# Sparse attention in one stream of a two-model program: scores from row halves of the array, values stationary, features on partitions

## The chip, the cores and the metric

The program runs on one core of a Trainium2 chip. The metric is the device time of one execution in microseconds (us). The kernel before took 1988.86 us in the median of 3 runs (1982.52 to 1991.17).

The engines by the names that the profile uses: PE is the matrix engine (PEld is its weight load), DVE the vector engine, ACT the scalar engine, POOL the general engine, SP the queue that issues most loads. PSUM is the memory that PE writes, in banks of 512 fp32 columns by 128 partitions.

## The reference

Two transformer blocks run one after the other on 256 tokens of width 1024. The second block has two layers, and in each of them three mixers read the same input: a gated linear attention, an RWKV recurrence and a sparse attention with 8 query heads and 2 key groups of 4 heads each. Their outputs, 256, 256 and 512 wide, stand side by side and are multiplied by `w_out`. Cut to what matters, the sparse attention is

```
o = gate0 * softmax(q k_cmp) v_cmp        # 15 compressed keys per group
  + gate1 * softmax(q k_s, causal) v_s    # "s"
  + gate2 * softmax(q k_w, causal) v_w    # "w"
```

With 256 tokens both of the last two branches are plain causal attention over all keys, so "s" and "w" are the same work on other keys and values. Head dimension is 64.

## The kernel before

Everything is kept in fp32. A product with a weight matrix is done in three matmuls on operands split in a high and a low part; products inside the mixers are true fp32 matmuls, which the trace shows as two passes each. The kernel is written with named pools of tiles, and a scheduler puts the instructions of all streams of a stage into one fixed order per engine; each engine then works strictly through its list and waits where an operand isn't ready. So the three mixers of a layer are woven into one list of PE instructions, and a stage of a layer ends with the product with `w_out` (`dense`, lines 215 to 217).

The stage is called "m2" in the table `SCOPES`: it gives the number of buffers of each tag, per stream (R is RWKV, G the gated attention, N the sparse attention), and the PSUM banks. Score banks of N are the two banks "d", which `dense` uses too; the transposed probabilities go through "n" for the first 128 tokens and "q" for the others; sums of the values go to the one bank "o".

The names that matter here:

- `nsa_in` makes the keys `N["kT"]`: 64 features of group 0 on partitions 0 to 63 and of group 1 on 64 to 127. The tile has a block of columns for each group, in which the other group's partitions are zero (`fill`), so that a whole-array matmul of the stacked queries of two heads with both blocks gives two heads' scores.
- `nsa_half` (line 1750) works on one half h of the tokens (128 queries). First comes the compressed branch: probabilities, transposed, times `vc`, in one matmul of 512 columns (line 1781), copied to `acc`.
- Then, for "s" and "w", it goes over groups of heads that fill one score bank: 4 heads of 128 keys in the first half, 2 heads of 256 keys in the second. Scores and the causal mask (a bf16 identity times a mask) go to the bank, DVE takes the maximum (line 556), ACT the exponentials with their sums (line 1802). `probs_T` transposes the unnormalised probabilities (line 750) and copies them to SBUF (line 118); each head's transposed block is then the stationary operand of a matmul with 64 columns of values. These last are the `po` rows of line 473; line 473 is the helper `Chain`, which keeps matmuls into one bank in order.
- When all 8 heads are done, DVE divides by the sums and multiplies by the gate (lines 1809, 1810, 1812), and POOL adds the result to `acc` (line 1813).
- `self.result` transposes `acc` (line 229) and splits it in high and low part (lines 232, 233), the operand of the product with `w_out`.

Of the kernel before, what the change touches and what calls it, by code (L numbers as in the profile page):

```python
# [18 lines left out]
AF = mybir.ActivationFunctionType  # L19
OP = mybir.AluOpType  # L20
# [8 lines left out]
class Core:  # L29
# [18 lines left out]
                     tC2="pC2", aC3="pC3", tC3="pC3", oO="o")),  # L48
        "m2": (dict(lb4R=1, s=11, op=3, ol=2, lb2N=5, lb2R0=3, lb2R1=3, b2R0=1, b2R1=1, lb4N=1, b05R=4, b05G=3, b05N=3, lb05N=2,
                     lb4G=2, b2G=5, lsR=5, lsG=1, lsN=1, sR=8, sG=6, sN=11, b1R=5, b1G=2, b1N=2, b2R=5, b2N=5, lb2G=8, lb2R=12),  # L50
                dict(g=1, r=2, q=1, aR0="r", tR0="r", aR1="q", tR1="g", n=1, o=1, d=2, aR="r", tR="r", oR="r", aG="g", tG="g",
# [946 lines left out]
class Mix2(Mix1):  # L998
# [108 lines left out]
    def mixer2(self, layer):  # L1107
        nc, I = self.nc, self.I
        get = self.norm_T(self.x, None)
        put, oget = self.operand(8, [("lb2G", 2), ("lb2R", 2), ("op", 4)])  # L1110

        self.result = lambda h, b0, nb, y: self.split_T(y, nb, lambda b, m: put(h, b0 + b, m))
        w = I["w_in_2"][layer]
        self.N = {}
        with self.on("N"):
            self.nsa_queries(get, w)
        for s, f, g in (("R", self.rwkv_in, self.rwkv), ("G", self.gla_in, self.gla), ("N", self.nsa_in, self.nsa)):
            with self.on(s):
                f(layer, get, w)
                with self.later(800 if s == "G" else 0):  # L1120
                    g(layer)

        def product(done):
            for n0 in (0, 512):
                self.dense(oget, I["w_out_2"][layer], n0, 512, lambda h, ps: done(h, n0, ps), order=(0, 2, 3, 1), apart=(("op", "ol"), None, ("lb4R", "lb4G"), None) if n0 else ())
        self.post("ln1", layer, "lb2R", product)
# [492 lines left out]
    def nsa_in(self, layer, get, w):  # L1619
        nc, I = self.nc, self.I  # L1620
        N = self.N

        kT = self.l(1024)
        self.fill(kT, 0.0)
        N["kT"] = kT.rearrange("p (n g t) -> p n g t", n=2, g=2)
        vs = self.l(512)
# [13 lines left out]
        def keys_T(h, src, j):  # L1640
            ro = rotated(h, src)
            pt = self.p("t")
            nc.tensor.transpose(pt[:, :128], ro, self.ident)
            for g in range(2):
                self.evac(N["kT"][64 * g:64 * g + 64, j, g, h * 128:(h + 1) * 128], pt[64 * g:64 * g + 64, :128])

# [103 lines left out]
    def nsa_half(self, h, kc, vc):  # L1750
# [27 lines left out]
        nc.tensor.transpose(pt[:, :128], pr, self.ident)  # L1778
        self.evac(pT, pt[:, :128])
        po = self.p("o")  # L1780
        nc.tensor.matmul(po, pT, vc, start=True, stop=True)
        acc = self.t(512)
        self.evac(acc, po)

        nk = 128 * (h + 1)
        per = 512 // nk
        for j, n in enumerate("sw"):
            po = self.p("o")
            och = Chain(self)
            sums = self.t(8)  # L1790
            for a in range(0, 8, per):

                heads = [(c // 2, c % 2) for c in range(a, a + per)]
                ps, sv, nmax, pr, pv = self.open_scores(per, nk)
                ch = Chain(self)
                for i in range(0, per, 2):
                    ch(sv[:, i:i + 2], qv[:, heads[i][0]], N["kT"][:, j, :, :nk], stop=False)
                    ch(sv[:, i:i + 2, nk - 128:], self.ident_b, self.cb["causal"][:, None, :].to_broadcast([128, 2, 128]), start=False)
                self.largest(sv, nmax)
                for i, (c, g) in enumerate(heads):  # L1800
                    c += 4 * g
                    nc.scalar.activation(pv[:, i], sv[:, i], AF.Exp, bias=nmax[:, i:i + 1], accum_out=sums[:, c:c + 1])
                pT = self.probs_T(h, [pv[:, i] for i in range(per)])
                for i, (c, g) in enumerate(heads):
                    s = slice((4 * g + c) * 64, (4 * g + c) * 64 + 64)
                    for b in range(h + 1):
                        och(po[:, s], pT[i, b], N["v"][n][b][:, rows(g)], start=(b == 0), stop=(b == h))
            r = self.t(8)
            nc.vector.reciprocal(r, sums)
            nc.vector.tensor_tensor(r, r, gate[:, :, 1 + j], op=OP.mult)  # L1810
            tmp = self.t(512)
            nc.vector.tensor_tensor(eight(tmp), eight(po), r[:, :, None].to_broadcast([128, 8, 64]), op=OP.mult)
            nc.gpsimd.tensor_tensor(acc, acc, tmp, op=OP.add)
        self.result(h, 4, 4, acc)


class Net(Mix2):
# [32 lines left out]
    "rwkv_g2_2", "rwkv_k_k_2", "rwkv_k_a_2", "rwkv_r_k_2", "rwkv_ln_w_2", "rwkv_ln_b_2", "nsa_pos_k_2",  # L1850
    "nsa_pos_v_2", "nsa_wk1_2", "nsa_wk2_2", "nsa_wv1_2", "nsa_wv2_2", "w_out_2", "ln1_w_2", "ln1_b_2",
    "ffn_w_down_2", "ln2_w_2", "ln2_b_2",
# [3 lines left out]
def gate_up(g, u):  # L1856
# [4 lines left out]
    both = both.transpose(*range(n), n + 3, n, n + 2, n + 1, n + 4, n + 5, n + 6)  # L1861
    return np.ascontiguousarray(both).reshape(*both.shape[:n + 3], 1024)


# [30 lines left out]
```

## Time and profile before

| what | value |
|---|---|
| median of 3 runs | 1988.86 us |
| the profiled execution, its own time | 1985.36 us |
| its span | 1983.7 us |
| PE busy | 1906.5 us (96%) |
| DVE busy | 1257.2 us (63%) |
| ACT busy | 1005.7 us (51%) |
| POOL busy | 191.4 us (10%) |
| granted TensorE clock, mean | 0.993 |

The span runs from the first instruction to the last; the time of the execution has 1.7 us around it. Time of a PE instruction is read from the start of one row to the start of the next, since its own duration holds a tail that overlaps the next one's start. In a row such as `128*64 128x128 f32` the first pair is the part of the array in use (rows by columns), the second the output. The stage of layer 0 whose order changes lies between about 1232 and 1352 us, that of layer 1 between about 1652 and 1773 us.

### The profile page before, as it was taken

Reading aid. Unit: us, or ns where it says so; the run is one execution under the profiler, and the core shown is the slowest. Engines: PE = TensorE matmul, PEld = TensorE weight load, DVE = VectorE, ACT = ScalarE, POOL = GpSimd, SP = SyncE. Lnnn points to the kernel's source line nnn. Section 1 sums busy time; section 2 is a strip of 40 time slices with the busy share of each in tenths; the row PEclk is TensorE's granted clock in tenths of the full one; section 3 lists DMA queues with packets and bytes.
Section 4 is the critical chain, followed back from the end, with each engine's and each line's share of the span. In section 5 each row is a group of like instructions: output and inputs, shape, how many; then the busy total and the mean of one; then the engine's idle time right before and its main releaser. Section 6 shows DMA issues by size and latency. Waiting matters only on the chain.

```text
span 1983.7 us, 34147 instructions
## 1 busy us (share of the span) xinstructions
PE 1906.5 (96%) x13548; PEld 1698.5 (86%) x13548; DVE 1257.2 (63%) x2007; ACT 1005.7 (51%) x1607; POOL 191.4 (10%) x270
## 2 busy tenths in 40 slices
PE   8999999899999999898999999998999999998998
PEld 7997788799989987677999788877998787878996
DVE  5665865766566656676666557666555767576555
ACT  5544655555445545665554445543454455444542
POOL 0000401000000001320000012310000213210000
PEclk9999999999999999999999999999999999999999
DMA  7666443466656656234566654313666745025664
GB/s 239 194 214 214 140 149 105 126 195 195 197 192 193 195 189 191 94 108 138 171 192 194 201 150 126 110 44 120 199 192 191 184 143 158 1 86 176 197 191 138
DMA packets 158641, 319.09 MB, mean 161 GB/s; under 512 B 28944, under 2 KB 49681, under 8 KB 158481
## 3 DMA queue, kind: packets, MB, share of 16 engines
q1 hardware_dynamic: 157888, 315.79, 51.6%
q8 instruction: 106, 1.74, 0.4%
q0 software_dynamic: 160, 0.52, 0.1%
q10 hardware_dynamic: 432, 0.60, 0.1%
q14 instruction: 55, 0.44, 0.1%
HBM read 315.82 MB, written 1.05 MB: 160 GB/s over the span
## 4 chain that ended last, share of the span: by engine, by line
PE 51%; issue 4%; DVE 3%; ACT 1%; DMA 0%; SPq 0%; POOL 0%; DVEq 0%; POOLq 0%; ACTq 0%
PE pd L473 23%; PE pd L216 5%; PE pd L215 5%; PE pd L217 5%; PE po L473 2%; PE ppC L473 1%; DVE wl L158 1%; PE pg L1240 1%; PE pg L473 1%; PE pt L509 0%; PE pr L1516 0%; PE pq L1516 0%; PE pq L1525 0%; PE pt L229 0%; PE pq L1521 0%
## 5 line engine op out<-in xcount | busy, mean ns | idle before, releaser
L158 DVE TENSOR_TENSOR wl<-wr,wh 128x1024 fp32r<-128x1024 f32 (+2 forms) x557 | 677.3, 1218 | 390.2 <-PE pd L473 133.9
L157 ACT ACTIVATE wh<-wr 128x1024 fp32r<-128x1024 f32 (+2 forms) x557 | 584.6, 1051 | 552.9 <-PE pd L473 206.9
L473 PE MATMUL pd<-opX,wl 128*128 128x256 f32 x2112 | 584.3, 277 | 2.2 <-DVE s L241 1.0
L473 PE MATMUL pd<-olX,wh 128*128 128x256 f32 x2112 | 584.4, 277 | 0.3 <-DVE olX L233 0.2
L473 PE MATMUL pd<-opX,wh 128*128 128x256 f32 x2112 | 583.7, 277 | 0.0
L473 PEld LDWEIGHTS pd<-opX,wl 128*128 128x128 f32 x2112 | 397.4, 188 | 3.1 <-ACT opX L232 2.2
L473 PEld LDWEIGHTS pd<-olX,wh 128*128 128x128 f32 x2112 | 397.8, 188 | 0.7 <-DVE olX L233 0.7
L473 PEld LDWEIGHTS pd<-opX,wh 128*128 128x128 f32 x2112 | 397.6, 188 | 0.0
L216 PE MATMUL pd<-wl,op 128*128 128x512 f32 (+5 forms) x984 | 375.6, 382 | 3.3 <-DVE wl L158 3.1
L217 PE MATMUL pd<-wh,op 128*128 128x512 f32 (+5 forms) x984 | 372.1, 378 | 0.0
L215 PE MATMUL pd<-wh,ol 128*128 128x512 f32 (+5 forms) x984 | 354.4, 383 | 3.0 <-DVE ol L233 1.7
L216 PEld LDWEIGHTS pd<-wl,op 128*128 128x128 f32 x984 | 185.5, 189 | 38.3 <-DVE wl L158 5.8
L215 PEld LDWEIGHTS pd<-wh,ol 128*128 128x128 f32 x984 | 184.6, 188 | 37.7 <-DVE ol L233 1.9
L217 PEld LDWEIGHTS pd<-wh,op 128*128 128x128 f32 x984 | 185.6, 189 | 32.5
L350 DVE TENSOR_TENSOR b<-pd,b 128x256 f32<-128x256 f32 x132 | 55.9, 424 | 62.2 <-ACT b L349 44.2
L242 POOL TENSOR_TENSOR ls<-s,cf 128x1 f32<-128x1 f32 (+2 forms) x30 | 25.4, 848 | 721.5 <-DVE s L241 721.5
L242 POOL TENSOR_TENSOR s<-s,cf 128x1 f32<-128x1 f32 (+2 forms) x22 | 23.0, 1048 | 428.3 <-DVE s L241 426.9
L473 PE MATMUL pd<-op,wl 128*128 128x256 f32 x208 | 58.5, 281 | 5.9 <-DVE lb2R L1316 4.4
L349 ACT ACTIVATE b<-b 128x256 f32<-128x256 f32 x88 | 36.8, 418 | 46.6 <-DVE b L348 46.6
L473 PE MATMUL pd<-ol,wh 128*128 128x256 f32 x208 | 58.1, 279 | 0.0
L473 PE MATMUL pd<-op,wh 128*128 128x256 f32 x208 | 57.9, 278 | 0.0
L354 DVE TENSOR_TENSOR ol<-b,op 128x512 fp32r<-128x512 f32 x66 | 45.4, 688 | 18.0 <-ACT op L353 18.0
(513 smaller groups left out, 2272.9 us busy)
## 6 DMA issues: line engine op xcount, KB each, us to landing
wr<-in_ffn_gu_dram SPq DMA_DIRECT2D x264, 512.0 KB, 4.1
wr<-in_ffn_w_down_dram SPq DMA_DIRECT2D x132, 512.0 KB, 3.6
wr<-in_w_in_dram SPq DMA_DIRECT2D x45, 512.0 KB, 4.5
wr<-in_ab_w_in_dram SPq DMA_DIRECT2D x24, 512.0 KB, 4.0
wr<-in_xm_w_kv_dram SPq DMA_DIRECT2D x16, 512.0 KB, 3.6
wr<-in_w_out_dram SPq DMA_DIRECT2D x16, 512.0 KB, 3.7
wr<-in_ab_w_out_dram SPq DMA_DIRECT2D x8, 512.0 KB, 3.5
wr<-in_xm_w_q_dram SPq DMA_DIRECT2D x8, 512.0 KB, 4.0
```

The lines of the kernel that those rows point to most:

```text
L157: nc.scalar.activation(hi, raw, AF.Copy)
L158: nc.vector.tensor_tensor(lo, raw, hi.bitcast(F32), op=OP.subtract)
L215: nc.tensor.matmul(o, xl, wh[:, k], start=first, stop=False)
L216: nc.tensor.matmul(o, xh, wl[:, k], start=False, stop=False)
L217: nc.tensor.matmul(o, xh, wh[:, k], start=False, stop=last)
L242: self.pow = nc.gpsimd.tensor_tensor(r, a, self.mhalf[:, :n], op=OP.pow)
L349: nc.scalar.activation(s, s, AF.Silu)
L350: nc.vector.tensor_tensor(y[:, b * 256:b * 256 + 256], ps[:, 256:], s, op=OP.mult)
L354: nc.vector.tensor_tensor(lo, yv, hi.bitcast(F32), op=OP.subtract)
L473: i = self.k.nc.tensor.matmul(out, lhsT, rhs, start=start, stop=stop, skip_group_check=skip)
L1240: nc.tensor.matmul(ps[rows(n), 4 * h + 2 * a:4 * h + 2 * a + 2], z[:, a, s], zq[:, a, :, s], start=True, stop=True)
```

## The change

- `nsa_in` no longer fills a zeroed tile for the keys: the tile holds 64 features of group 0 and of group 1 on the two halves of the partitions, and one copy writes it.
- Scores: for each head one matmul with 64 rows of the array (its group's half), 128 or 256 columns, in place of one whole-array matmul for two heads. Two score banks are opened, one for each group.
- The probabilities are divided by their sums and multiplied by the gate before they are transposed (`weigh`, a DVE product of 512 columns), with a reciprocal and a product of 2 or 4 sums for each bank.
- Values are the stationary operand, 64 columns of the array (the half of the group), and the transposed probabilities move, 512 or 256 columns at a time. All three branches add into one bank "o" whose partitions are features; `acc`, the product at the end of each branch, the POOL additions and the four transposes of `result` are gone. The bank is split into high and low part directly (`split`).
- The rows of `w_out` are put in the order of the new operand when the inputs are laid out.
- The table gives N one more buffer of two kinds and drops the 1024-wide one.

In the new file the lines of `nsa_half` move: line 1811 is the transpose that was line 750, and lines 1805, 1806 and 697 the reciprocal, the product of the sums and `weigh`.

```diff
-        "m2": (dict(lb4R=1, s=11, op=3, ol=2, lb2N=5, lb2R0=3, lb2R1=3, b2R0=1, b2R1=1, lb4N=1, b05R=4, b05G=3, b05N=3, lb05N=2,
-                     lb4G=2, b2G=5, lsR=5, lsG=1, lsN=1, sR=8, sG=6, sN=11, b1R=5, b1G=2, b1N=2, b2R=5, b2N=5, lb2G=8, lb2R=12),
+        "m2": (dict(lb4R=1, s=11, op=3, ol=2, lb2N=6, lb2R0=3, lb2R1=3, b2R0=1, b2R1=1, b05R=4, b05G=3, b05N=3, lb05N=2,
+                     lb4G=2, b2G=5, lsR=5, lsG=1, lsN=1, sR=8, sG=6, sN=11, b1R=5, b1G=2, b1N=2, b2R=5, b2N=6, lb2G=8, lb2R=12),
...
-        kT = self.l(1024)
-        self.fill(kT, 0.0)
-        N["kT"] = kT.rearrange("p (n g t) -> p n g t", n=2, g=2)
+        N["kT"] = self.l(512).rearrange("p (n t) -> p n t", n=2)
...
-            for g in range(2):
-                self.evac(N["kT"][64 * g:64 * g + 64, j, g, h * 128:(h + 1) * 128], pt[64 * g:64 * g + 64, :128])
+            self.evac(N["kT"][:, j, h * 128:(h + 1) * 128], pt[:, :128])
...
         po = self.p("o")
-        nc.tensor.matmul(po, pT, vc, start=True, stop=True)
-        acc = self.t(512)
-        self.evac(acc, po)
+        pov = po.rearrange("p (i t) -> p i t", i=4)
+        och = Chain(self)
+        for i in range(4):
+            for g in range(2):
+
+                och(pov[rows(g), i], vc[:, (4 * g + i) * 64:(4 * g + i) * 64 + 64], pT, start=(i == 0), stop=False, skip=True)
...
-            for a in range(0, 8, per):
-
-                heads = [(c // 2, c % 2) for c in range(a, a + per)]
-                ps, sv, nmax, pr, pv = self.open_scores(per, nk)
-                ch = Chain(self)
-                for i in range(0, per, 2):
-                    ch(sv[:, i:i + 2], qv[:, heads[i][0]], N["kT"][:, j, :, :nk], stop=False)
-                    ch(sv[:, i:i + 2, nk - 128:], self.ident_b, self.cb["causal"][:, None, :].to_broadcast([128, 2, 128]), start=False)
-                self.largest(sv, nmax)
-                for i, (c, g) in enumerate(heads):
-                    c += 4 * g
-                    nc.scalar.activation(pv[:, i], sv[:, i], AF.Exp, bias=nmax[:, i:i + 1], accum_out=sums[:, c:c + 1])
-                pT = self.probs_T(h, [pv[:, i] for i in range(per)])
-                for i, (c, g) in enumerate(heads):
-                    s = slice((4 * g + c) * 64, (4 * g + c) * 64 + 64)
-                    for b in range(h + 1):
-                        och(po[:, s], pT[i, b], N["v"][n][b][:, rows(g)], start=(b == 0), stop=(b == h))
-            r = self.t(8)
-            nc.vector.reciprocal(r, sums)
-            nc.vector.tensor_tensor(r, r, gate[:, :, 1 + j], op=OP.mult)
-            tmp = self.t(512)
-            nc.vector.tensor_tensor(eight(tmp), eight(po), r[:, :, None].to_broadcast([128, 8, 64]), op=OP.mult)
-            nc.gpsimd.tensor_tensor(acc, acc, tmp, op=OP.add)
-        self.result(h, 4, 4, acc)
+            for a in range(0, 4, per):
+                S = [self.open_scores(per, nk) for g in range(2)]
+                chains = [Chain(self) for g in range(2)]
+                for i in range(per):
+                    for g in range(2):
+                        chains[g](S[g][1][:, i], qv[rows(g), a + i], N["kT"][rows(g), j, :nk], start=(i == 0), stop=False, skip=True)
+                st = []
+                for g, (ps, sv, nmax, pr, pv) in enumerate(S):
+                    chains[g](sv[:, :, nk - 128:], self.ident_b, self.cb["causal"][:, None, :].to_broadcast([128, per, 128]),
+                              start=False, skip=True)
+                    self.largest(sv, nmax)
+                    sums = self.t(per)
+                    for i in range(per):
+                        nc.scalar.activation(pv[:, i], sv[:, i], AF.Exp, bias=nmax[:, i:i + 1], accum_out=sums[:, i:i + 1])
+                    nc.vector.reciprocal(sums, sums)
+                    nc.vector.tensor_tensor(sums, sums, gate[:, 4 * g + a:4 * g + a + per, 1 + j], op=OP.mult)
+                    self.weigh(pv, sums)
+                    pt = self.p("t")
+                    st.append(self.t(512))
+                    for m, (b, i) in enumerate((b, i) for b in range(h + 1) for i in range(per)):
+                        nc.tensor.transpose(pt[:, m * 128:(m + 1) * 128], pv[:, i, b * 128:(b + 1) * 128], self.ident)
+                    self.evac(st[-1], pt)
+                for b in range(h + 1):
+                    for g in range(2):
+                        och(pov[rows(g), a:a + per], N["v"][n][b][:, rows(g)], st[g][:, b * per * 128:(b + 1) * per * 128],
+                            start=False, stop=(n == "w" and b == h), skip=True)
+        self.split(self.put, h, 4, pov)
```

The order of the instructions changes in the second part of the two m2 stages alone, and there on PE, DVE, ACT and POOL; SP's list is the same. PE's list in layer 0, second half of the tokens, branch "w", before: `pd` with 512 columns are the scores, `pd<-cb` the mask, `pq` the transposes of the probabilities, `po` the products with the values, `pr` another stream.

```order
L473 MATMUL pd_14641<-lb4N_14011,lb2N_12395 128x512
L473 LDWEIGHTS cb
L473 MATMUL pd_14641<-cb 128x2x128
L1469 MATMUL pr_13432<-lb2R_12988,lb2R_12991 64x64 x8
L473 MATMUL po_14601<-lb2N_14013,b2N_14612 128x64 x4
L750 MATMUL pq_14630<-cf,b2N_14623 128x128 x4
L473 MATMUL pd_14660<-lb4N_14011,lb2N_12395 128x512
L473 LDWEIGHTS cb
L473 MATMUL pd_14660<-cb 128x2x128
L473 MATMUL po_14601<-lb2N_14013,b2N_14631 128x64 x4
L750 MATMUL pq_14649<-cf,b2N_14642 128x128 x4
```

PE's list at the same place, after: `pd_14638` and `pd_14641` are the score banks of group 0 and group 1, `pq_14612` and `pq_14627` the transposes of the two banks before.

```order
L473 MATMUL pd_14638<-lb2N_14008,lb2N_12392 128x256 x2
L473 LDWEIGHTS cb
L473 MATMUL pd_14638<-cb 128x2x128
L1811 MATMUL pq_14612<-cf,b2N_14595 128x128 x4
L473 MATMUL po_14497<-b2N_14613,lb2N_14009 64x256
L473 MATMUL pd_14641<-lb2N_14008,lb2N_12392 128x256 x2
L473 LDWEIGHTS cb
L473 MATMUL pd_14641<-cb 128x2x128
L1811 MATMUL pq_14627<-cf,b2N_14598 128x128 x4
L473 MATMUL po_14497<-b2N_14628,lb2N_14009 64x256
L473 MATMUL po_14497<-b2N_14613,lb2N_14009 64x256
L473 MATMUL po_14497<-b2N_14628,lb2N_14009 64x256
```

The scores of the two groups stand apart, with mask, transposes and a product with values between them, and each `po` row that reads a tile (`b2N_14613`, `b2N_14628`) stands right behind the transposes that fill it. Before, a score, its mask or another stream's work stood between.

PE's list where the stage of layer 0 ends, before: `po` is the last product with values, `pq<-cf` the transposes of `acc`, `pd` the product with `w_out` for the first (`pd_14702`) and second half of the tokens (`pd_14703`), `op` and `ol` the operand from N.

```order
L473 MATMUL po_14601<-lb2N_14013,b2N_14669 128x64 x4
L215 MATMUL pd_14703<-wh_14706,lb2G_12391 128x512
L216 MATMUL pd_14703<-wl_14707,lb2G_12388 128x512
L217 MATMUL pd_14703<-wh_14706,lb2G_12388 128x512
L215 MATMUL pd_14703<-wh_14706,lb2G_12391 128x512
L216 MATMUL pd_14703<-wl_14707,lb2G_12388 128x512
L217 MATMUL pd_14703<-wh_14706,lb2G_12388 128x512
L229 MATMUL pq_14685<-cf,b2N_14515 128x128 x4
L216 MATMUL pd_14702<-wl_14743,op_12390 128x512
```

And after (`pd_14694` and `pd_14695` are the two halves now):

```order
L217 MATMUL pd_14694<-wh_14734,op_12387 128x512
L215 MATMUL pd_14694<-wh_14752,lb2R_12389 128x512
L473 MATMUL po_14497<-b2N_14672,lb2N_14009 64x256
L473 MATMUL po_14497<-b2N_14657,lb2N_14009 64x256
L473 MATMUL po_14497<-b2N_14672,lb2N_14009 64x256
L215 MATMUL pd_14695<-wh_14716,ol_12390 128x512
L216 MATMUL pd_14695<-wl_14717,op_12387 128x512
L217 MATMUL pd_14695<-wh_14716,op_12387 128x512
```

The transposes are gone, and the first row behind the last product reads the low part of that product's own result.

## Rows read from the trace of the kernel before

**Rows 1.** The page: span, and busy time of each engine.

```profile
span 1983.7 us, 34147 instructions
PE 1906.5 (96%) x13548; PEld 1698.5 (86%) x13548; DVE 1257.2 (63%) x2007; ACT 1005.7 (51%) x1607; POOL 191.4 (10%) x270
```

**Rows 2.** Stretches: length, busy PE, PEld, DVE, ACT, POOL (instructions), clock, DMA.

```profile
1232.50:1284.00 51.50, 51.50 (x499) 42.39 (x499) 35.20 (x86) 28.45 (x60) 17.39 (x26) 1.00 0.35 112
1303.00:1344.00 41.00, 39.98 (x327) 29.89 (x327) 29.19 (x102) 17.92 (x52) 6.81 (x6) 1.00 0.17 53
1724.00:1765.00 41.00, 39.98 (x326) 29.81 (x326) 29.39 (x103) 18.26 (x52) 6.79 (x6) 1.00 0.16 52
```

**Rows 3.** PE in order of time: start, length, instruction [idle before, releaser].

```profile
1277.32 0.60 PE L473 MATMUL pd<-lb4N,lb2N 128*128 128x256 f32 x2
1277.75 0.27 PE L473 MATMUL pd<-cb 128*128 128x256 bf16 x1
...
1316.30 1.10 PE L473 MATMUL po<-lb2N,b2N 128*128 128x64 f32 x8 [0.71 <-ACT b2N L118]
1317.24 0.61 PE L750 MATMUL pq<-cf,b2N 128*128 128x128 f32 x4
1317.69 1.02 PE L473 MATMUL pd<-lb4N,lb2N 128*128 128x512 f32 x2
1318.55 0.27 PE L473 MATMUL pd<-cb 128*128 128x256 bf16 x1
1318.66 1.00 PE L473 MATMUL po<-lb2N,b2N 128*128 128x64 f32 x8
1319.50 0.61 PE L750 MATMUL pq<-cf,b2N 128*128 128x128 f32 x4
```

**Rows 4.** The same view, a block in which two row halves work.

```profile
1190.39 0.48 PE L1381 MATMUL pr<-b1R,b1R 64*128 64x256 f32 x1
1190.40 0.48 PE L1382 MATMUL pr<-lb2R,b1R 64*128 64x256 f32 x1
1190.71 0.38 PE L1381 MATMUL pr<-b1R,b1R 64*128 64x256 f32 x1
...
1191.15 0.38 PE L1382 MATMUL pr<-lb2R,b1R 64*128 64x256 f32 x1
1191.46 0.39 PE L473 MATMUL pd<-ol,wh 128*128 128x256 f32 x1
```

**Rows 5.** The same view, blocks of column halves and whole array in turn.

```profile
1284.83 1.09 PE L1240 MATMUL pg<-lb4G,b2G 128*64 128x128 f32 x16
1285.86 1.10 PE L1543 MATMUL pr<-b1R,lb2R 128*128 128x64 f32 x8
1286.89 0.66 PE L1548 MATMUL pr<-lb2R,lb2R 128*64 128x128 f32 x8
1287.48 1.16 PE L1525 MATMUL pq<-lb2R,b2R 128*128 128x128 f32 x8
```

**Rows 6.** The same view, the end of the stage in layer 0.

```profile
1343.09 1.10 PE L473 MATMUL po<-lb2N,b2N 128*128 128x64 f32 x8 [0.31 <-ACT b2N L118]
...
1346.40 0.66 PE L229 MATMUL pq<-cf,b2N 128*128 128x128 f32 x4 [0.75 <-POOL b2N L1813]
1347.48 0.50 PE L216 MATMUL pd<-wl,op 128*128 128x512 f32 x1 [0.42 <-DVE wl L158]
```

**Rows 7.** Single lines: duration in ns, least/median/most, first and last start.

```profile
L697 DVE TENSOR_TENSOR b2C<-b2C,sC x20: 684/692/694, 372.4 to 936.6; 128x512 f32<-128x512 f32 x20
L1809 DVE RECIPROCAL sN<-sN x8: 195/202/204, 1291.7 to 1760.7; 128x8 f32<-128x8 f32 x8
L1810 DVE TENSOR_TENSOR sN<-sN,lb05N x8: 158/162/166, 1292.7 to 1761.1; 128x8 f32<-128x8 f32 x8
L1812 DVE TENSOR_TENSOR b2N<-po,sN x8: 691/692/692, 1297.3 to 1765.1; 128x512 f32<-128x512 f32 x8
L118 ACT ACTIVATE b2N<-pq x8: 590/597/602, 1315.7 to 1342.4; 128x512 f32<-128x512 f32 x8
```

More of the change, by code (lines that the diff above doesn't have):

```diff
@@ L1112, in mixer2 @@
         self.result = lambda h, b0, nb, y: self.split_T(y, nb, lambda b, m: put(h, b0 + b, m))
+        self.put = put
         w = I["w_in_2"][layer]
@@ L1787, in nsa_half @@
         for j, n in enumerate("sw"):
-            po = self.p("o")
-            och = Chain(self)
-            sums = self.t(8)
-            for a in range(0, 8, per):
-                heads = [(c // 2, c % 2) for c in range(a, a + per)]
-                ps, sv, nmax, pr, pv = self.open_scores(per, nk)
-                ch = Chain(self)
-                for i in range(0, per, 2):
-                    ch(sv[:, i:i + 2], qv[:, heads[i][0]], N["kT"][:, j, :, :nk], stop=False)
-                    ch(sv[:, i:i + 2, nk - 128:], self.ident_b, self.cb["causal"][:, None, :].to_broadcast([128, 2, 128]), start=False)
-                self.largest(sv, nmax)
-                for i, (c, g) in enumerate(heads):
-                    c += 4 * g
-                    nc.scalar.activation(pv[:, i], sv[:, i], AF.Exp, bias=nmax[:, i:i + 1], accum_out=sums[:, c:c + 1])
-                pT = self.probs_T(h, [pv[:, i] for i in range(per)])
-                for i, (c, g) in enumerate(heads):
-                    s = slice((4 * g + c) * 64, (4 * g + c) * 64 + 64)
-                    for b in range(h + 1):
-                        och(po[:, s], pT[i, b], N["v"][n][b][:, rows(g)], start=(b == 0), stop=(b == h))
@@ L1850 @@
     "rwkv_g2_2", "rwkv_k_k_2", "rwkv_k_a_2", "rwkv_r_k_2", "rwkv_ln_w_2", "rwkv_ln_b_2", "nsa_pos_k_2",
-    "nsa_pos_v_2", "nsa_wk1_2", "nsa_wk2_2", "nsa_wv1_2", "nsa_wv2_2", "w_out_2", "ln1_w_2", "ln1_b_2",
+    "nsa_pos_v_2", "nsa_wk1_2", "nsa_wk2_2", "nsa_wv1_2", "nsa_wv2_2", "ln1_w_2", "ln1_b_2",
     "ffn_w_down_2", "ln2_w_2", "ln2_b_2",
@@ L1862, in gate_up, with out_rows @@
     return np.ascontiguousarray(both).reshape(*both.shape[:n + 3], 1024)
+def out_rows(w):
+    w = np.asarray(w)
+    n, _, c = w.shape
+    last = w[:, 512:].reshape(n, 2, 4, 64, c).transpose(0, 2, 1, 3, 4).reshape(n, 512, c)
+    return np.ascontiguousarray(np.concatenate([w[:, :512], last], 1))
 def kernel(**inputs):
@@ L1882 @@
     add("ffn_gu_2", gate_up(inputs["ffn_w_gate_2"], inputs["ffn_w_up_2"]))
+    add("w_out_2", out_rows(inputs["w_out_2"]))
     add("constants", CONST)
```

## The prediction, made before the change was run

> **What bounds the kernel now.** I read the page first: PE is busy for 1906.5 of 1983.7 us, the next engine for 1257.2 [rows 1]. Then the busy time by stretch over the part of the m2 stages in which the order changes: PE is busy for all of 51.50 us between 1232.5 and 1284.0, and for 39.98 of 41 us in the last part of the stage, in layer 1 as in layer 0 [rows 2]. There DVE has 29 of 41 us of work, ACT 18, the loads 17% of the DMA engines. So these stages last as long as PE's list, and a change is worth what it takes from or adds to that list, plus the places in which PE waits. Last I read PE's list in order of time, row by row, which gives the price of a pass and of the waits.
>
> **Prices.** All are start to start. A whole-array fp32 matmul is two passes: with 512 columns both take 0.86 us (1317.69 to 1318.55), 0.43 a pass; with 256 columns 0.43, 0.215 a pass; four matmuls of 64 columns, eight passes, take 0.84 to 0.94 us, 0.11 a pass; four transposes 0.45; a mask of 256 columns 0.11 [rows 3]. The price of a pass follows the moving columns from 128 up (0.11, 0.215, 0.43) and doesn't fall below 0.11.
>
> A pass on half of the array costs what one on the whole costs, but two in different halves run together: two row halves of 256 columns start 0.01 us apart, eight passes in four pairs, and the next pair 0.2 us later [rows 4]. Two column halves do the same: sixteen passes last 1.03 us up to the next row, eight 0.59, so eight more cost 0.44, 0.11 a pair [rows 5].
>
> A change of the array's shape costs extra. The block of eight passes in column halves lasts 0.59 for 0.44 of pairs, 0.15 more [rows 5]; the row halves 1.07 us for four pairs of 0.215, 0.21 more [rows 4]. The Trainium skill says in "TensorEngine Tiling (Array Packing)", section Key Properties, that a change of tiling mode drains the engine; it has no price for it. By that rule, which the trace bears out with 0.15 and 0.21 us, this change has a cost that its count of columns doesn't show.
>
> **The change on PE, both layers together.**
> - Scores before: 16 matmuls of 256 columns (16 x 0.43) and 16 of 512 (16 x 0.86), 20.6 us. After: 32 of 128 columns on 64 rows (32 x 2 x 0.11 = 7.0) and 32 of 256 (32 x 0.43 = 13.8), 20.8, and 0.5 less because one bank pair in the first half stands side by side in the list. Nothing is gained: each head's 64 rows cost what the zeros cost before, and in the second half of the tokens the two groups stand apart in PE's list, with the mask and transposes between them, so no pair forms.
> - Masks: the same columns, 3.5 us.
> - Products with values before: 24 blocks of four, 24 x 0.9 = 21.5 us. After: 8 of 512 columns (8 x 0.86 = 6.9) and 32 of 256 (32 x 0.43 = 13.8). Of the 32, the list has runs of three with the halves in turn, where one finds its partner in the other half: 8 in all, 8 x 0.43 = 3.4 less. Together 17.3: 4.2 saved.
> - Compressed branch: 4 matmuls of 512 columns, 3.5 us, become 32 of 128 columns in pairs, 16 x 0.22 = 3.5.
> - 16 transposes of `result` go: 4 x 0.45 = 1.8 saved.
>
> That is 6.3 us less (0.3, 4.2 and 1.8). Against it stand the shape changes. Before, all of N's blocks here use the whole array. After, a bank goes from 64 rows (scores) to whole (mask, transposes) to 64 columns (values). I counted the changes over PE's whole list by the rows and columns that each matmul uses: 360 before, 417 after; 54 of the 57 new ones are into or out of 64 rows. At 0.15 to 0.21 they cost 8.6 to 12.0 us; a change between two half shapes stands nearer to 0.15, so I take 0.17 and 9.7 us. PE's list gets 3.4 us longer.
>
> **The change on the waits.** In the list after, the products with values stand right behind the transposes that fill their operand at 4 places in each layer. The copy between them takes 0.60 us on ACT [rows 7]. Before, 0.97 us of score and mask covered it (1317.69 to 1318.66, no idle), and where it was not covered PE waited 0.71 and 0.31 us [rows 3, 6]. Four waits of 0.65 are 2.6 us a layer, against 1.0 before: 1.6 more in each, 3.2 in all. Below, such a wait can cost only what the copy leaves open, 0.5; above, a copy queued behind other work on ACT would cost over 1.
>
> At the end of the stage, before, PE waited 0.75 us for POOL's addition, did the transposes, and waited 0.42 us [rows 6]. After, the first row behind the last product needs its low part: a copy of 0.60 and a subtraction of 0.69 (priced by lines 118 and 1812) with hardly anything between, 1.4 to 1.5 us, in place of 1.2: 0.6 for both layers.
>
> DVE gets longer: for each of 12 banks a layer a reciprocal (0.20), a product (0.16) and `weigh`, whose own line stood in the first block with 0.69 us [rows 7], 12.6 us; the four endings of a branch go (4 x 1.05 = 4.2). So 8.4 us more in each layer, some 6 of them in the 41 us that hold 29 of DVE's work. I cost that at nothing in the likeliest case: 35 of 41 us still fits, and between a bank's mask and its transposes the list after has, by the prices above, 4 us and more of other PE work nearly everywhere, under which maximum, exponentials and the 1.05 us of new steps can go on. ACT and POOL lose work (the copies of `acc`, half of the key copies, the additions), which nothing waits for except at the end.
>
> Sum: -6.3 + 9.7 + 3.2 + 0.6 = 7.2 us. On the profiled execution, 1985.36, that gives 1992.6; the median of the runs lies 3.5 us above the profiled one, so I forecast 1996.1 against 1988.86, 0.4% longer. Two versions within 0.5%, 9.9 us, can't be told apart here.
>
> **Rivals.**
> - DVE ends the stage. The waits of PE then come from `weigh` and not from the copies. For it: DVE has 29 of 41 us now [rows 2], its list is strictly in order, and the recurrence of the other stream has its steps between. Against it: PE waits for DVE nowhere in these 41 us except for 0.42 at the end [rows 6]. It decides once DVE's work a bank (1.05 more) shifts a transpose past its place. If half of the 8.4 us comes through to PE, both layers lose 8.4 more: 2004.5, slower.
> - Shape changes are cheaper than counted, because a wait of PE at the same place hides them or the drained time is shared. For it: before, waits and changes stood at the same places in few cases only, so the rows don't show it; after, there are some. At half the price, 4.9 less: 1991. At none: 1986.4. No change either way.
> - The halves pair up after all. The Trainium skill says in the page named, section When to Use Tiling, that a contraction of 64 or a swap of the stationary and the moving operand with 64 columns gives up to twice the speed, and this change does both. It would need every score and every product with values to find its partner: scores 10.4 for 20.3 us, values 10.4 for 17.3, 16.8 less than my sum, 1979.3. The trace has such pairs [rows 4, 5], but only for neighbours in the list; PE's list puts the halves apart, and what the copy of one group's probabilities is waiting for doesn't bring them together.
>
> **How the numbers follow.** The forecast has 0.50; its own range is 1990 to 2002, from the two ends of the shape change and of the copies, and some 0.08 of it lie above 1998.8. DVE has 0.23, cheap changes 0.20, full pairs 0.07. So slower by over 0.5% 0.31, within 0.5% 0.62, faster by over 0.5% 0.07. The range for the time is 1984 to 2008: it leaves out the full pairs and the worst of DVE, and holds the 4 us by which runs of one kernel differ.
>
> **What would show it.** In the profile after: rows of 64*128 in the second half of the tokens that follow each other at 0.215 us a pass without a partner, and about 0.2 us more before the mask; idle before `po` of 0.5 to 0.8 us, released by ACT line 118, four times a layer; idle of about 1.5 us before the first low-part row behind the last product; DVE near 35 us in the last 41 of a stage. Pairs of 64*128 rows 0.01 us apart in most banks would make the forecast wrong downwards, and idle before the transposes of the probabilities that DVE line 697 releases would make it wrong upwards.

## The result, and the profile after

The changed kernel takes 2014.63 us in the median of 4 runs (2011.3 to 2025.22), the kernel before 1988.2 in 4 runs: ratio 1.0135, 95% interval 1.0105 to 1.0166. The forecast was 1996, its range ended at 2008. The profiled execution took 2012.31 us, 26.95 more than that of before.

The page of the changed kernel, span and busy time, which answers to [rows 1]: PE is busy 15.0 us longer in a span 26.9 us longer.
```profile
span 2010.6 us, 34109 instructions
PE 1921.5 (96%) x13532; PEld 1698.3 (84%) x13532; DVE 1271.8 (63%) x2055; ACT 1000.2 (50%) x1595; POOL 180.2 (9%) x260
```
The two m2 stages of the kernel before, each between the same two PE instructions in both kernels; the columns are those of [rows 2].
```profile
1232.80:1352.90 120.10, 117.90 (x1057) 92.71 (x1055) 77.06 (x210) 61.67 (x160) 30.11 (x39) 1.00 0.22 70
1652.10:1774.70 122.60, 117.78 (x1060) 93.80 (x1059) 78.83 (x211) 62.15 (x159) 26.23 (x36) 1.00 0.23 73
```
The same stretches of the changed kernel, its three stretches at a clock of 0.50 (the first reads 0.51 because its ends are rounded), and 41 us that end 9 us before the first stage does, as those in [rows 2].
```profile
1230.50:1356.90 126.40, 119.00 (x1049) 89.82 (x1048) 84.88 (x234) 59.01 (x154) 25.00 (x37) 0.99 0.20 67
1656.90:1801.10 144.20, 134.38 (x1051) 98.44 (x1050) 86.18 (x235) 59.37 (x153) 22.28 (x35) 0.91 0.20 62
1338.20:1341.60 3.40, 3.40 (x11) 2.10 (x8) 2.68 (x8) 0.49 (x3) 0.00 (x0) 0.51 0.02 5
1751.20:1771.70 20.50, 20.50 (x103) 13.42 (x104) 10.27 (x35) 3.69 (x9) 1.01 (x1) 0.50 0.10 26
1778.60:1785.40 6.80, 6.03 (x18) 4.04 (x19) 2.50 (x7) 1.78 (x6) 0.00 (x0) 0.50 0.00 0
...
1307.00:1348.00 41.00, 35.69 (x262) 23.74 (x260) 30.30 (x99) 15.23 (x47) 3.56 (x3) 0.96 0.15 52
```
The stages are 27.9 us longer, the rest of the program 1.0 us shorter. Three parts are read from these rows. Idle time is length less busy PE: 2.2 and 4.8 us before, 7.4 and 9.8 after, 10.2 more. Time lost to the clock is half of PE's busy time at 0.50, which is 1.2 GHz in place of 2.4: 3.4, 20.5 and 6.03 us, so 15.0. What is left, PE's busy time less that loss, is called the list here, PE's work at full clock: 235.7 before, 238.4 after, 2.7 more. So over half of the 27.9 us is the clock, which no step of the prediction had. PE hardly waits at half clock (26.53 of 27.30 us busy in layer 1), and at full clock some waits might show there, so 15.0 is the most that a kept clock would have given back.

PE's waits in the stage of layer 0 of the kernel before: line waited for, us in total, times, longest.
```profile
PE po L473 <- ACT b2N L118: 1.0, 2, 0.7
PE pq L229 <- POOL b2N L1813: 0.7, 1, 0.7
PE pd L216 <- DVE wl L158: 0.4, 1, 0.4
```
The same of the changed kernel, layer 0 and then, behind the dots, lines of layer 1 that differ.
```profile
PE po L473 <- ACT b2N L118: 3.0, 4, 0.7
PE pd L215 <- DVE ol L693: 1.4, 1, 1.4
PE pq L1811 <- DVE sR L241: 0.8, 1, 0.8
PE pd L216 <- DVE wl L158: 0.6, 1, 0.6
PE pq L1811 <- DVE b2N L697: 0.4, 1, 0.4
PE pd L473 <- ACT b2N L1804: 0.3, 1, 0.3
PE pd L215 <- ACT b2N L1804: 0.3, 1, 0.3
...
PE po L473 <- ACT b2N L118: 2.6, 4, 0.7
PE pq L1811 <- DVE b2N L697: 1.0, 2, 0.7
PE pd L473 <- ACT b2N L1804: 0.5, 2, 0.3
PE pq L1811 <- DVE sR L1096: 0.3, 1, 0.3
```
The four waits for copies and the one at the end, behind `split` (line 693), are there as foretold; those before the transposes (line 1811) and those for banks "d" that the exponentials (line 1804) still read are new.

PE of the changed kernel in order of time, where the clock falls in layer 1 (at 1751.2).
```profile
1744.30 0.66 PE L1811 MATMUL pq<-cf,b2N 128*128 128x128 f32 x4
1745.70 0.65 PE L473 MATMUL po<-b2N,lb2N 128*64 128x256 f32 x2 [0.75 <-ACT b2N L118]
1746.61 1.13 PE L473 MATMUL pd<-lb2N,lb2N 64*128 64x256 f32 x4 [0.27 <-ACT b2N L1804]
1747.67 0.28 PE L473 MATMUL pd<-cb 128*128 128x256 bf16 x1
...
1749.89 4.84 PE L473 MATMUL pg<-lb2G,lb2G 128*128 128x64 f32 x31 [0.34 <-DVE lb2G L233]
...
1756.48 2.07 PE L473 MATMUL pd<-lb2N,lb2N 64*128 64x256 f32 x4
1758.48 0.40 PE L473 MATMUL pd<-cb 128*128 128x256 bf16 x1
```
Four passes of 64 rows take 1.06 us at 1746.61 and 2.00 at 1756.48, the same work at half the clock. Ahead of the fall stand waits and blocks that use half of the array. Which of the two does it is the question of the experiments.

### The profile page after: what moved, and what is told of

Read it like the earlier page. It is cut to its first block, busy times and chain, and to the rows that moved or that the text cites. A ratio compares the mean times of both kernels' runs of the same rounds, so it can differ in the third digit from the quotient of the medians.

```text
span 2010.6 us, 34109 instructions
## 1 busy us (share of the span) xinstructions
PE 1921.5 (96%) x13532; PEld 1698.3 (84%) x13532; DVE 1271.8 (63%) x2055; ACT 1000.2 (50%) x1595; POOL 180.2 (9%) x260
## 4 chain that ended last, share of the span: by engine, by line
PE 50%; DVE 4%; issue 4%; ACT 1%; DMA 0%; POOL 0%; SPq 0%; DVEq 0%; ACTq 0%; POOLq 0%
PE pd L473 23%; PE pd L215 5%; PE pd L216 5%; PE pd L217 5%; PE po L473 1%; PE ppC L473 1%; DVE wl L158 1%; PE pg L1241 1%; PE pg L473 1%; PE pr L1517 0%; PE pq L1526 0%; PE pq L1517 0%; PE pt L509 0%; PE pq L1522 0%; PE pt L229 0%
```

## The experiments

Theory "idle": the waits lower the clock. Theory "partial array": the passes that use half of the array do, above all the 64-row scores. The table has all kernels, by the reckoning above for both stages together (us), from one profile each; clocks are those of the timed runs, the mean of a whole run. The kernel before had 0.988 to 0.996 in 35 runs. The edits are shown shortened.

| kernel | ratio to before, interval | clock | length | idle | busy at 0.50 | list |
|---|---|---|---|---|---|---|
| before | | 0.988-0.996 | 242.7 | 7.0 | 0 | 235.7 |
| after | 1.0135 (1.0105-1.0166) | 0.979-0.989 | 270.6 | 17.2 | 29.9 | 238.4 |
| e1 filler in the waits | 1.0083 (1.0053-1.0113) | 0.987-0.992 | 261.7 | 12.1 | 6.5 | 246.4 |
| e2 whole-array scores | 1.0076 (1.0052-1.0100) | 0.989-0.993 | 260.8 | 18.5 | 10.2 | 237.2 |
| e3 groups side by side | 1.0082 (1.0054-1.0110) | 0.983-0.990 | 259.1 | 24.3 | 19.7 | 224.9 |
| e4 values written later | 1.0098 (1.0059-1.0137) | 0.986-0.989 | 270.5 | 17.1 | 29.8 | 238.5 |
| e5 row-half scores alone | 1.0119 (1.0061-1.0176) | 0.981-0.993 | 265.0 | 7.5 | 33.6 | 240.7 |
| e6 values forced later | 1.0201 (1.0164-1.0237) | 0.973-0.981 | 280.5 | 17.9 | 52.8 | 236.2 |
| e7 no weights | 1.0102 (1.0059-1.0146) | 0.984-0.988 | 260.5 | 11.1 | 26.1 | 236.4 |
| e8 after again | 1.0132 (1.0102-1.0162) | 0.983-0.987 | 270.5 | 17.3 | 29.9 | 238.3 |
| e9 e5 with filler | 1.0083 (1.0054-1.0112) | 0.990-0.994 | 257.5 | 8.0 | 0 | 249.5 |
| e10 e2, values in pairs | 1.0087 (1.0063-1.0111) | 0.986-0.990 | 261.3 | 26.5 | 12.8 | 228.5 |
| e11 e10, weights on POOL | 1.0116 (1.0085-1.0147) | 0.981-0.991 | 268.0 | 28.5 | 21.6 | 228.7 |
| e12 e5, scores in pairs | 1.0104 (1.0078-1.0130) | 0.985-0.988 | 263.4 | 17.0 | 23.6 | 234.6 |

**e1: filler in the waits.** For each bank of the second half of the tokens, tied behind its transposes:
```
+ for k in range(2):
+     och(po, zeros_bf16, causal_4x128, start=False, stop=False)
  och(pov[rows(g), a:a + per], N["v"][n][b][:, rows(g)], st[g], ...)
```


> The changed kernel with filler on PE: behind the transposes of each bank of probabilities of the last 128 tokens, ahead of the product with values that waits for their copy, two bf16 matmuls of 512 columns add a product with zeros to the bank of sums (16 places in two layers, 0.43 us each by the mask's 0.11 per 256 columns). Theory 'idle': the half clock of the two m2 stages (30 us at 0.50 in the changed kernel's profile, 15 us lost) follows from PE's waits of 0.75 us for the copies. Then less than 8 us at 0.50 are left between the start of the first m2 stage and the end of the second, and the time falls to 2001 to 2006 although 7 us of work are added, of which the waits take 3. Rival 'partial array': it follows from the passes that use half of the rows or columns, whether PE waits or not. Then some 30 us at 0.50 stay and the time is 2017 to 2020.

Both stages:
```profile
1242.60:1367.50 124.90, 120.69 (x1064) 90.10 (x1062) 84.77 (x234) 58.94 (x154) 24.98 (x37) 1.00 0.21 67
1668.10:1804.90 136.80, 128.95 (x1068) 94.90 (x1067) 86.66 (x235) 59.35 (x153) 21.99 (x35) 0.98 0.20 66
```
PE has 8 us more in its list, yet the stages are 9 us shorter: 6.5 us at 0.50 are left of 29.9. The half clock is as "idle" foresaw, but the time, 2009.83 us beside 1992.49 of the kernel before there, missed its 2001 to 2006. The profile has another 17.1 us at 0.50 from 807.7, in a part of the program that no edit touches. The filler shortens waits and adds whole-array work, so this run alone doesn't part the two theories.

**e2: scores on the whole array.**
```
- qv[rows(g), a + i], N["kT"][rows(g), j, :nk]
+ qv[:, a + i],       N["kT"][:, j, g, :nk]      # zeros in the other group's rows
```


> The changed kernel with the scores on the whole array again: a tile with zeros for the other group, 128 rows instead of 64, the same number of passes and columns; values, normalisation and waits as in the changed kernel. (The tile of 1024 columns takes the place of one buffer of 512 of each of two kinds.) Theory 'partial array': the half clock goes, less than 8 us at 0.50 in the m2 stages, and with some 50 shape changes fewer at 0.17 (8 us) the time is 1991 to 1996. Theory 'idle': PE's waits stay, so some 30 us at 0.50 stay; only the shape changes go, 2005 to 2010. If shape changes were hidden behind waits anyway, 2012 to 2016.

Both stages:
```profile
1234.20:1362.20 128.00, 119.65 (x1049) 90.70 (x1048) 83.89 (x234) 59.97 (x158) 25.62 (x35) 0.99 0.20 66
1661.90:1794.70 132.80, 122.62 (x1051) 92.76 (x1050) 86.47 (x235) 60.49 (x157) 21.43 (x32) 0.97 0.21 68
```
Idle time is no less than in the changed kernel (8.4 and 10.2), and two thirds of the half clock are gone: waits alone don't bring it. No theory's numbers came: 10.2 us at 0.50 stay where "partial array" had under 8, and 2007.35 us is above its 1991 to 1996. The shape changes that go were counted as some 50 and 8 us of list. Row by row, PE's list in the trace changes shape 418 times in place of 443: only 25 go, since other changes take the place of those at the row halves. At 0.17 that is 4.3 us; 1.2 came.

**e3: the groups side by side.** One chain for the scores of both banks, and `for g in (1, 0)` for scores and products.

> The changed kernel with the two groups put side by side in PE's list: the scores of both banks in one chain, group 1 first, and the products with values in the order group 1, group 0, so that all four stand behind the later copy and run in pairs of column halves. Theory: values pair in all 8 double banks of the last 128 tokens (0.43 us less each, 3.4 in all), scores in about half of their passes (3.4 less), PE's list is 7 us shorter. 'Idle': the score banks are no longer worked on in turn, so the waits for maximum and exponentials grow by more than the list shrinks, and the half clock stays (30 us or more): 2010 to 2025. 'Partial array': pairs use the whole array, the half clock falls under 15 us: 1995 to 2003.

The list is 13.5 us shorter, twice what was counted, since the products pair everywhere: they take 12.0 us, start to start at full clock, in place of 20.3. But idle grows by 7 us: PE now waits for both score banks at once (up to 1.6 us for the exponentials). With 19.7 us at 0.50 and 2008.79 us beside 1992.49 it lies between the two theories.

**e4 and e6: the waits for copies.** In e4 the products of a double bank are written one step later in the program; in e6 they are tied there:
```
+ add_manual_dep(product(g=0), next_mask(g=1)); add_manual_dep(product(g=1), next_transposes(g=0))
```


> The changed kernel with each double bank's products with values written one step later, behind the scores and transposes of the next, so that the copy has been done when PE comes to the product. Passes, columns and shape changes as in the changed kernel. Theory 'idle': the waits for ACT line 118 fall from 5.6 us in two layers under 1.5, and the half clock goes with them (under 8 us at 0.50): 1993 to 1999. 'Partial array': only the waits go, 2008 to 2011. If the order of the other streams shifts so that PE waits for DVE instead, idle in the two stages stays above 15 us and the time above 2010.

> The changed kernel with the products of a double bank tied behind the next double bank's work in PE's list: the first of group 0 behind the next mask of group 1, the first of group 1 behind the next transposes of group 0 (writing them later in the program alone left the order as it was). Passes and columns are unchanged. The waits for ACT line 118 fall from 5.6 us in two layers to 1.5 or less (the last bank of a stage keeps its own). Theory 'both' and 'idle': half clock in the m2 stages under 10 us, 12 to 17 us under the changed kernel, 6 to 12 over the one before. 'Partial array alone': only the waits go, 5 us under the changed kernel. If the products, moved, delay the next scores or the transposes, idle stays at 15 us and so does the clock.

In e4 the scheduler put the products where they had been (four waits for line 118 in each layer, 5.6 us), so e4 is a second look at the changed kernel. In e6 no wait for line 118 is left, but others stand in its place, for exponentials and for steps of DVE, so neither expected time came, 5 or 12 to 17 us under the changed kernel. Both stages of e6, and the longest stretch at 0.50 of all profiles:
```profile
1233.90:1363.00 129.10, 122.47 (x1048) 91.62 (x1047) 84.96 (x234) 58.87 (x154) 24.59 (x37) 0.96 0.20 65
1663.00:1814.40 151.40, 140.10 (x1051) 103.24 (x1050) 87.32 (x235) 59.56 (x153) 22.15 (x35) 0.84 0.19 59
1754.60:1799.00 44.40, 39.89 (x167) 26.02 (x168) 23.87 (x77) 10.80 (x34) 3.29 (x3) 0.50 0.12 44
```
With the idle time of the changed kernel (17.9) it loses 26 us to the clock in place of 15, and its median is 2031.44 beside 2018.27 of the changed kernel (e8) and 1988.89 of the one before. Idle time alone doesn't set the loss.

**e5: row-half scores alone, on the kernel before.**
```
- ch(sv[:, i:i + 2], qv[:, i], N["kT"][:, j, :, :nk])              # two heads, zeros
+ ch(sv[:, i], qv[rows(g), a + i], N["kT"][rows(g), j, :nk])       # one head, 64 rows
```


> The kernel before with one part of the change: scores from row halves of the array (64 rows, each group its own bank, the keys without zeros); probabilities are stationary, sums and gates come at the end, as before. PE's waits should be those of before (7 us idle in the two m2 stages). Theory 'partial array alone': the clock falls as in the changed kernel, 20 us and more at 0.50 in the m2 stages and a clock of 0.988 or less, 12 to 18 us over the kernel before. Theory 'both' (the clock falls where PE waits and its rows use part of the array, since with whole-array scores and the same waits, in the run before this one, 10 us at 0.50 were left of 30): clock as before, 0.991 to 0.993, less than 8 us at 0.50 there, and the time within 5 us of the kernel before. The shape changes, 8 us by the price in the prediction, would come on top if they cost what was counted; the run with whole-array scores says they don't.

Both stages, the stage of layer 0 up to the first fall of the clock, that fall, and the long stretch at 0.50:
```profile
1236.60:1373.40 136.80, 133.70 (x1085) 106.36 (x1084) 77.91 (x210) 60.84 (x156) 30.43 (x41) 0.89 0.20 62
1678.90:1807.10 128.20, 123.79 (x1087) 99.41 (x1086) 79.93 (x211) 60.78 (x155) 27.10 (x39) 0.99 0.22 70
1236.60:1320.00 83.40, 83.40 (x840) 68.42 (x840) 51.81 (x142) 40.86 (x105) 24.83 (x37) 1.00 0.21 69
1320.00:1323.40 3.40, 3.40 (x12) 1.68 (x12) 1.86 (x11) 1.54 (x2) 0.14 (x1) 0.50 0.00 0
1326.80:1350.70 23.90, 23.90 (x107) 18.34 (x106) 9.12 (x23) 6.48 (x20) 1.26 (x1) 0.50 0.19 66
```
PE in order of time ahead of the first fall, and at the second:
```profile
1316.99 3.74 PE L473 MATMUL pg<-lb2G,lb2G 128*128 128x64 f32 x32
...
1324.63 0.89 PE L750 MATMUL pq<-cf,b2N 128*128 128x128 f32 x4 [1.14 <-ACT b2N L1799]
1325.46 1.13 PE L473 MATMUL pd<-lb2N,lb2N 64*128 64x256 f32 x4
1326.52 0.28 PE L473 MATMUL pd<-cb 128*128 128x256 bf16 x1
1326.64 1.61 PE L473 MATMUL po<-lb2N,b2N 128*128 128x64 f32 x8
...
1329.03 2.07 PE L473 MATMUL pd<-lb2N,lb2N 64*128 64x256 f32 x4
1331.04 0.39 PE L473 MATMUL pd<-cb 128*128 128x256 bf16 x1
```
This decides against the waits. PE waits as little as in the kernel before (7.5 us against 7.0), the clock falls first after 83.40 us of the stage in which PE was busy throughout, and PE is busy for all of the 23.90 us at half clock; its one wait of 1.14 us lies between the two falls. The Trainium skill, "TensorE: Matmul & The Clock Gate", section "HAM oscillation — how this bites in real kernels", has idle gaps of PE as what drops the clock; by that alone this stage would have kept it, and the measurement decides. Values stationary, the products and the weights aren't in this kernel, so the fall needs none of them. In three of four runs: 2017.9 to 2022.16 us at 0.981 to 0.985, more than the 12 to 18 us over that were expected, and one of 1998.24 at 0.993, so with the clock kept the part costs 9 us (one run), without it some 30.

It doesn't show the row halves alone, for two reasons. PE's list is 5.0 us longer at full clock, and what a change of shape adds to a block counts as busy. And the scheduler has woven the other streams anew in layer 0: the second block of `pg` rows of the gated attention starts 80.4 us into the stage, right ahead of the first fall. In the changed kernel it starts 76.7 us into it, in e2 95.2 and before 94.3, with this row:
```profile
1327.13 2.41 PE L473 MATMUL pg<-lb2G,lb2G 128*128 128x64 f32 x20
```
In layer 1, where it starts 101.0 us into the stage of e5 and 95.9 before, e5 has only 2.9 us at 0.50. So e5 leaves the order of the other streams as a rival, though the changed kernel, with the early block as well, has only 3.4 us at 0.50 in layer 0. For layer 1 the pair to compare is e2 and the changed kernel (90.6 and 93.0, idle 10.2 and 9.8): 6.8 us at 0.50 with whole-array scores, 26.5 with row halves.

**e7: no weights.** `reciprocal`, the product with the gate and `weigh` are left out.

> The changed kernel without the reciprocal, the product with the gate and the product with the probabilities: the sums of the two large branches are left unnormalised, 12.6 us less of DVE work in each layer and 1.05 us less between exponentials and transposes of a bank. If DVE's new work makes the waits (rival of the prediction), idle of the two m2 stages falls from 17 to 10 us or less, PE no longer waits for DVE at the transposes, and with the half clock the time is 10 to 18 us under the changed kernel. If the waits are those for the copies alone, idle falls by 2 to 3 us and the time by 2 to 5, since the copies stand behind the transposes as before.

Both stages, and the stretch at 0.50 in layer 0:
```profile
1237.30:1362.70 125.40, 124.96 (x1041) 92.55 (x1039) 71.25 (x190) 57.66 (x152) 24.46 (x37) 0.93 0.20 66
1668.60:1803.70 135.10, 124.47 (x1052) 93.76 (x1051) 76.36 (x200) 59.33 (x153) 21.75 (x35) 0.95 0.21 69
1310.30:1327.40 17.10, 17.10 (x82) 10.87 (x82) 5.25 (x18) 4.83 (x14) 1.02 (x1) 0.50 0.19 63
```
In layer 0 idle goes from 7.4 to 0.4 us, the waits for copies with it: there DVE's new work makes the waits, by its time or through the order, which changes too. In layer 1 idle is 10.6, with one wait of 6.0 us for a DVE step of the gated attention (line 1273) that the new order put late, so the share of DVE isn't settled there. The median, 2011.87, is 6 us under the changed kernel (e8), less than the 10 to 18 expected. And in a stage with 0.4 us of idle PE has 17.1 us at 0.50: again it isn't the waits.

**e8: the changed kernel again.**

> The changed kernel once more, beside the three others on the same chip: 1.2 to 1.5% over the kernel before, clock 0.983 to 0.989, some 30 us at 0.50 in the two m2 stages, most of it in layer 1, if the fall of the clock belongs to the kernel; under 10 us there if the profile of the changed kernel was an odd one.

2018.27 us beside 1988.89, and in the profile the same stretch of 20.5 us at 0.50, starting 94.3 us into the stage of layer 1 both times (1758.5 here). The fall belongs to the kernel.

**e9: e5 with filler.** In the score banks of the second half of the tokens, behind the scores:
```
+ for k in range(2 * h):
+     ch(ps, zeros_bf16, causal_4x128, start=False, stop=False)
```


> The kernel with scores from row halves alone (the run before, which had no more idle time than the kernel before, 7.5 us, but 30.7 us at 0.50 in the stage of layer 0), with filler: for each bank of scores of the last 128 tokens two bf16 matmuls of 512 columns over the whole array add a product with zeros to the bank, 16 banks, 0.43 us each, 7 us of work more. Theory 'partial array': whole-array work between the row halves keeps the clock; under 8 us at 0.50 are left in the m2 stages, the clock is 0.990 or more, and although work is added the time falls from some 30 to between 10 and 18 us over the kernel before. Rival (the clock falls for the shape changes or for what stands around the scores): it stays at 0.986 or less and the time is 33 to 40 us over.

Both stages:
```profile
1233.40:1360.90 127.50, 123.67 (x1100) 97.85 (x1099) 78.09 (x211) 60.88 (x156) 29.71 (x41) 1.00 0.20 66
1662.90:1792.90 130.00, 125.79 (x1104) 99.36 (x1101) 79.30 (x211) 60.53 (x155) 27.21 (x39) 1.00 0.22 69
```
Idle is as in e5 (8.0), the list 8.8 us longer, and no time at 0.50 is left; all seven runs have 0.990 or more, where one of e5's four had. With more work on PE the two stages are 7.5 us shorter. The medians go the same way, 2009.73 beside 1992.63 (17 us over) where e5 was 31 over, but the intervals of the two ratios overlap. The 64-row rows and their shape changes are all still there, and the other streams stand as in e5 (the `pg` block 81.2 us into the stage), so the work between them is what brought the clock back. That it has to use the whole array wasn't tested: no run has filler on half of it.

**e10 and e11: a better version looked for.** e10 is e2 with the products in the order group 1, group 0; e11 has the weights' product on POOL.

> Whole-array scores, with values stationary as in the changed kernel, and the products with values in the order group 1, group 0, so that they run in pairs of column halves. PE's list should be 3.4 us shorter than with whole-array scores alone (16 pairs in place of 8 in two layers, 0.43 us each); clock as there, 0.991; if the later copy costs nothing more, 11 to 13 us over the kernel before, else 15 to 18.

> The kernel of the run before this one with the product of probabilities and weights on POOL (1.27 us for 128x512 by a POOL addition of the kernel before) in place of DVE (0.69). If DVE's load makes the waits of PE (without that work the first m2 stage had 0.4 us idle in place of 7.4), idle in the two stages falls from some 18 to under 12 us and the time to 4 to 9 us over the kernel before. If it is the length of the way from exponentials to transposes, idle grows by 0.6 us for each of some 8 uncovered banks, to 22 us or more, and the time to 16 to 22 over.

e10's list is 8.7 us shorter than e2's where 3.4 were counted, 7 shorter than that of before, and idle takes 8 of it back. These aren't waits for the later copy, which get fewer (2.9 us in place of 5.6), but for exponentials (8.3 in place of 1.5) and `weigh` (4.9 in place of 1.2). 2009.96 beside 1992.63. e11: 28.5 us idle, 2014.63. DVE has 10 us less to do there and PE waits no less, so DVE's load isn't what PE waits for. That it is the length of the way from exponentials to transposes fits, but idle grew by 2.0 us over e10 and not by 0.6 for each of 8 banks, so it isn't shown. e11's profile has 17.1 us at 0.50 from 808.8 too, as e1's has. No version here beats the kernel before.

**e12: row halves in pairs.** e5 with both groups' scores in one chain, tied behind the exponentials of both banks.

> The kernel with scores from row halves alone, with the scores of both groups in one chain of PE's list that starts when both banks are free, so that most of the 64-row passes have a partner in the other half. PE's list is 6 to 9 us shorter than with the row halves apart (64 columns halves of 0.215 us and 128 of 0.11). If rows of half an array lower the clock for the half that stands empty, pairs keep it: under 10 us at 0.50, clock 0.990 or more; the time is then within 8 us of the kernel before, or below it if the waits for both banks cost less than 6 us. If it is less work in the same time that lowers it, pairs with waits are no better: 20 us or more at 0.50 and 10 to 25 us over.

Both stages:
```profile
1235.00:1364.90 129.90, 123.55 (x1084) 98.65 (x1083) 77.92 (x210) 60.53 (x156) 29.71 (x41) 0.95 0.21 67
1666.20:1799.70 133.50, 122.85 (x1087) 97.99 (x1086) 79.66 (x211) 60.67 (x155) 26.97 (x39) 0.96 0.21 69
```
The list is 6.1 us shorter than e5's, but 23.6 us at 0.50 stay. So pairs as they can be had here don't save the clock. But they do the same work in less time and then wait (17.0 us idle in place of 7.5), so whether a partner in the other half would save it without the waits isn't shown.

## Why the prediction was wrong

- **The step that failed** is the sum itself: it priced every row at the clock at which it had been read (1.00 in [rows 2]) and had no term for the clock. "Nothing is gained: each head's 64 rows cost what the zeros cost before" holds for the price of a pass and not for what follows: the matmuls with zeros were whole-array work, and in the kernel without them the clock falls. That is 15.0 of the 27.9 us in the profile. That waits don't bring it is shown by e5 and e7; that the zeros kept most of it, by e2 (ten runs at 0.989 to 0.993; 6.8 us at 0.50 in place of 26.5 in layer 1, where idle and order are much the same); and that other whole-array work beside the row halves does so too, by e1 and e9. No rival had it either.
- **PE's list**, +3.4: measured +2.7, so the sum came out. The price of a change of shape is seen in its place (four 64-row passes take 1.06 us up to the mask, for 0.86). But that it may be multiplied by the count isn't shown. By the traces the list has 57 changes more, as counted; e2 has 25 fewer than the changed kernel and saves 1.2 us, 4.3 at 0.17, and e5 has 42 more than the kernel before and pays 5.0, 7.1 at 0.17. At e5's 0.12 the 57 cost 6.8 us and not 9.7, so other terms must be short by about as much as this one was over: that the sum fits is in part luck. The order of the other streams changes as well, and these runs don't part the two.
- **The waits for copies**, +3.2: 5.6 us against 2.0, +3.6, four a layer of 0.65 to 0.75. Right in place and size. The end of the stage, +0.6: 1.4 and 0.6 in place of 0.7 and 0.4, +1.8 for both layers; I had put the second wait into the first.
- **DVE at nothing**: wrong. The transposes wait 2.5 us in both layers for DVE, and banks "d" 1.4 for exponentials. The rival "DVE ends the stage" had the right place and the wrong reason: DVE is busy for 30.30 of 41 us in layer 0, 1.1 more than before [rows 2], not 35, so it is no bound there; PE waits for a result that comes late, and without the new steps it doesn't (e7 in layer 0). With 0.7 of other waits these make 10.0 of the 10.2 us more of idle time, where 3.8 were forecast.
- **The pairs** (1979.3): the list does shrink by 8.7 and 13.5 us where the groups are put side by side (e10, e3), but PE waits 7 to 8 us longer, above all for exponentials and `weigh`, and with row halves the clock is low as well.
- Without the loss of clock the same sum gives 1985.36 + 2.7 + 10.2 - 1.0 = 1997.3 for the profiled execution, an estimate that leaves the waits as they are. It is inside the range, 4.7 above the 1992.6 that was forecast for it.

**What stays open**: why the clock falls in layer 1 of the changed kernel and in layer 0 of e5; what part the new order of the other streams has in it; why one run of e5 kept it; and how the loss divides between row halves, column halves and waits, since e2, e10 and e11, with whole-array scores, still have 10.2, 12.8 and 21.6 us at 0.50, more where idle is longer. Something besides PE's list has a share: around 808 us, where that list is the same row for row in the kernel before, in the changed one and in e1 and e11, the last two have 17.1 us at 0.50 in one piece, the first two no piece over 6.8.

## What to carry to other kernels

Before counting a matmul on half of the array as equal to one padded with zeros, ask what keeps TensorE's clock up in that stage: here putting the zeros back brought most of it back, and the loss of clock cost more than all new waits together (15.0 us against 10.2). Read the clock of a stretch beside its busy time, and test a suspected loss of clock by adding harmless whole-array work: if the half clock goes and the stage gets shorter, the clock was it. Where a division by sums is moved ahead of a transposition, price the longer way from bank to bank too: here the engine that does it had room, and PE waited all the same.

## What the runs showed of the hardware

- The granted clock fell to 0.50 in stretches in which PE was busy throughout (23.90 of 23.90 us in e5, 17.10 of 17.10 in e7), the first time in e5 after 83.40 us without a wait, and PE's rows then took twice as long (four 64-row passes 2.01 us in place of 1.06).
- The fall repeats with the list: the changed kernel showed 20.5 us at 0.50 at the same place in two profiles (e8), and e4, with nearly the same list, 20.5 us as well. It isn't certain: one of four runs of e5 had 0.993, the others 0.981 to 0.985.
- 16 blocks of two whole-array bf16 matmuls with zeros, 8.8 us of PE's list, removed 33.6 us at 0.50 (e5 to e9).
- Products in different column halves ran together where the list had them side by side: those with the values took 12.0 us in e3 and 20.3 in the changed kernel.
